# One weight block against a split activation on one Trainium2 core: two matmuls of unequal width, or three of equal width

## The chip, the core and the metric

The kernel runs on one core of a Trainium2 chip. A core has five engines that run their own instruction streams side by side and meet through semaphores: TensorE (PE in the profile; its weight loads have a row of their own, PEld), VectorE (DVE), ScalarE (ACT), GpSimd (POOL) and SyncE (SP, which here issues the transfers from memory). TensorE writes into PSUM, eight banks of 512 float32 columns in each of 128 partitions; everything else lives in SBUF. The metric is the time of one execution on the device, in microseconds (us), and lower is better.

## The reference, cut to what matters

Two decoder layers over 256 tokens with 1024 channels. Each layer is a SwiGLU feed-forward at half weight, a token mixing step, and a second feed-forward, each followed by a layer norm over `alpha * x + sublayer(x)`:

```python
def swiglu(x, w_gate, w_up, w_down):
    return (jax.nn.silu(x @ w_gate) * (x @ w_up)) @ w_down
...
for l in range(DEPTH):
    x = layer_norm(alpha * x + 0.5 * swiglu(x, ffn_w_gate[l, 0], ffn_w_up[l, 0], ffn_w_down[l, 0]), ...)
    u = x @ w_in                                   # conv mixer in layer 0, mLSTM in layer 1
    mix = jnp.concatenate([tok, xa], -1) @ w_out[l]
    x = layer_norm(alpha * x + mix, ...)
    x = layer_norm(alpha * x + 0.5 * swiglu(x, ffn_w_gate[l, 1], ffn_w_up[l, 1], ffn_w_down[l, 1]), ...)
```

The mixer of layer 0 is a gated short convolution, that of layer 1 an mLSTM; in both, a cross-attention into 256 memory tokens runs beside it and the two are concatenated. The feed-forward width is 2816. All of it is float32, and nearly all of the arithmetic is products of a [256, 1024] activation with a weight matrix that is used once.

## The kernel before, in words

To keep float32 accuracy in TensorE's fast float32 format, every operand is split into two exact parts: a rounded high part (ACT copies it, line 99) and the remainder (DVE subtracts, line 100). A product of two split operands is then three products: high by high, high by low and low by high. The weights stream in once from memory, in pieces of [128, 2048] (1 MB), and each piece is split on arrival into `wh` and `wl`; five pieces are held at a time.

There are two ways in which a product is laid out. With the activation stationary (`mm3`, lines 171 to 177), three matmuls of 512 columns each go into the same PSUM columns; the down products (`y`), the output projection (`yo`), the first groups of a feed-forward (`gx`) and the values (`v`) go this way. With the weights stationary (`mmw`, lines 179 to 182), the output comes out transposed, which is what the next product needs; the feed-forward's gate and up products (`gu`), the projections of the mixers (`cg`, `cx`, `cb`, `qkp`), the queries (`xq`) and the memory's keys (`kb`) go this way, a block of 128 by 128 weights at a time.

In `mmw` the activation's two parts lie side by side, 256 tokens each, so one matmul with the high weights covers both parts in 512 columns (line 181): the left half of the PSUM bank gathers high by high, the right half high by low. A second matmul of 256 columns adds the low weights' product to the left half (line 182). After eight such pairs, one for each 128 input channels, the two halves of the bank have to be added: `comb` (lines 184 to 187) lets ACT copy the right half into SBUF, and DVE adds the left half to it. ACT's Silu (line 297), DVE's product of gate and up (line 298) and the split of the result (lines 301 and 302) follow.

A feed-forward has 11 groups of 256 columns. For each of them two pieces hold gate and up, one piece the down weights; `gu_ws` runs four accumulations (`fc` is the half of the group, `m` is gate or up), each into a bank of its own, and the down product of the group before follows. The first group of the first feed-forward is walked chunk by chunk (`outer`), because it starts while its operands are still landing. Each conv, mLSTM or query projection (`proj_ws`) is two accumulations, with `comb` after each. Matmul outputs come from two pools of four PSUM banks, `mbank` and `ybank`; a fifth accumulation waits until the first one's bank has been read. A scheduler decides the order in which each engine's instructions stand, and semaphores are derived from the data; all engines take their instructions in that order.

Of the kernel before, what the change touches and what calls it, by code (L numbers as in the profile page):

```python
# [14 lines left out]
P = 128  # L15
T = 256
# [15 lines left out]
def trunk(ctx: ExitStack, tc: tile.TileContext, d, out):  # L32
# [18 lines left out]
    def mbank(name):  # L51
        return psm.tile([P, 512], F32, tag="mm", name=name)
# [118 lines left out]
    def mm3(o, a, b, start, stop):  # L171
        """o += a^T b with a, b in two exact parts."""
        ah, al = a
        bh, bl = b
        pe.matmul(o, ah, bh, start=start, stop=False)  # L175
        pe.matmul(o, ah, bl, start=False, stop=False)  # L176
        pe.matmul(o, al, bh, start=False, stop=stop)  # L177

    def mmw(bank, w, a, start, stop):
        """bank = [w_h^T a_h + w_l^T a_h | w_h^T a_l], a's parts side by side."""  # L180
        pe.matmul(bank, w[0], a.rearrange("p c t -> p (c t)"), start=start, stop=False)  # L181
        pe.matmul(bank[:, :T], w[1], a[:, 0], start=False, stop=stop)  # L182

    def comb(o, bank):
        """The sum of a bank's two halves."""
        act.activation(o, bank[:, T:], AF.Copy)  # L186
        dve.tensor_add(o, o, bank[:, :T])  # L187
# [76 lines left out]
    def ffn(l, j, xs_groups, i, last=False):  # L264
# [6 lines left out]
        def gu_ws(g, outer=False):  # L271
            w = [get("gu", l, j, g, 0), get("gu", l, j, g, 1)]
            new_h(g)
            banks = {}

            def mm(fc, m, k):
                if k == 0:
                    banks[fc, m] = mbank(f"gu{l}{j}_{g}_{fc}{m}")
                c0 = (k % 4) * 512 + m * 256 + fc * P
                wk = w[k // 4]  # L280
                mmw(banks[fc, m], (wk[0][:, c0:c0 + P], wk[1][:, c0:c0 + P]), cur["x"][:, k],
                    k == 0, k == KC - 1)

            if outer:
                for k in range(KC):
                    for fc in range(2):
                        for m in range(2):
                            mm(fc, m, k)
            for fc in range(2):
                t_ = tmp(f"s{l}{j}_{g}_{fc}")  # L290
# [89 lines left out]
    kvs = {}  # L380

    def mem_kv(mem):
        w = [get("kv", q) for q in range(4)]
        for l in range(2):
            kvs[l] = (consts.tile([P, 2, T], F32, name=f"kT{l}"), consts.tile([P, 2, T], F32, name=f"vm{l}"))
        for c in range(4):
            b = mbank(f"kb{c}")
            for k in range(KC):
                s = slice((k % 2) * D + c * P, (k % 2) * D + (c + 1) * P)
                wk = w[k // 2]  # L390
                mmw(b, (wk[0][:, s], wk[1][:, s]), mem[:, k], k == 0, k == KC - 1)
            comb(kvs[c // 2][0][:, c % 2], b)
# [20 lines left out]
    def proj_to(o, w, name):  # L413
        proj_ws(w, name, lambda c, b: comb(o[:, c * T:(c + 1) * T], b))

    class Xattn:
        def __init__(self, l, w, mix):
            self.l, self.mix = l, mix
            self.kT, self.v = kvs[l]
            self.qT = tmp(f"xqT{l}")  # L420
            self.p = {}

            def use(c, b):
                o = self.qT[:, c * T:(c + 1) * T]
                act.activation(o, b[:, T:], AF.Copy, scale=0.125)
                dve.scalar_tensor_tensor(o, b[:, :T], 0.125, o, op0=ALU.mult, op1=ALU.add)
            proj_ws(w, f"xq{l}", use)
# [84 lines left out]
    def conv_mixer(mix, between):  # L512
        for i in range(3):
            cg = tmp(f"cgs{i}")
            proj_to(cg, get("wc", 1 + 3 * i), f"cg{i}")
            between[i]()
            tt = tmp(f"ct{i}")
            proj_to(tt, get("wc", 2 + 3 * i), f"cx{i}")
            dve.tensor_mul(tt, cg, tt)
# [8 lines left out]
            bt = tmp(f"cb{i}")  # L528
            proj_to(bt, get("wc", 3 + 3 * i), f"cb{i}")
            dve.tensor_mul(r, r, bt)  # L530
# [9 lines left out]
    def mlstm_mixer(mix, i):  # L540
# [3 lines left out]
        # the output gate, natural; the input and forget gates ride along  # L544
# [21 lines left out]
        # gates as rows [head, t]  # L566
# [7 lines left out]
        def gate_rows():  # L574
# [5 lines left out]
            # log_sigmoid(f) = min(f, 0) - log1p(exp(-|f|)); ln(u) is corrected for u's rounding  # L580
# [12 lines left out]
            # running sums and maxima  # L593
# [17 lines left out]
        # decay weights, transposed: E[s, t] = exp(a_s - M_t) for t >= s  # L611
# [12 lines left out]
        # q and k, convolved, silu'd, transposed: [channel, q or k, chunk, t]  # L624
        qk = [hp.tile([P, 2, 2, T], F32, tag="h", name=f"qk{n}") for n in range(3)]

        def qk_piece(n):
# [3 lines left out]
            ut = tmp(f"qu{n}")  # L631

            def use(c, b):
# [8 lines left out]
            proj_ws(get("wm", 1 + n), f"qkp{n}", use)  # L642
# [15 lines left out]
        # h = num / max(|den|, exp(-m)), head norm  # L658
# [32 lines left out]
        # v, natural, with a column of ones after each head  # L691
# [91 lines left out]
def _layouts(i):  # L783
# [5 lines left out]
    def colmajor(w, width):  # L789
        """[1024, n*width] -> [n, 128, 8*width]: piece, k in chunk, chunk x column."""  # L790
# [44 lines left out]
```

## Time and profile before

| what | value |
|---|---|
| median of 3 runs | 1002.04 us (1001.4 to 1003.79) |
| profiled execution, first to last instruction | 1004.1 us, 0.2% above that median |
| busy: PE, PEld, DVE, ACT | 986.8, 834.7, 664.8, 530.1 us |
| PE matmuls | 5116, each with a weight load of its own |
| granted TensorE clock, mean | 0.991 |

The profile has one row for each group of like instructions: the line of the kernel, the engine, the operation, what it writes and reads, how many there are, the busy time, the mean of one and the idle time just before them. The end of a matmul is modelled and matmuls overlap, so the duration of one says little about how fast they follow each other. For that one reads the timeline, which gives the start of each instruction: the distance between two starts is what a matmul costs in a full queue. In the text below this distance is called a slot.

### The profile page before, as it was taken

Reading aid. Unit: us, or ns where it says so; the run is one execution under the profiler, and the core shown is the slowest. Engines: PE = TensorE matmul, PEld = TensorE weight load, DVE = VectorE, ACT = ScalarE, POOL = GpSimd, SP = SyncE. Lnnn points to the kernel's source line nnn. Section 1 sums busy time; section 2 is a strip of 40 time slices with the busy share of each in tenths; the row PEclk is TensorE's granted clock in tenths of the full one; section 3 lists DMA queues with packets and bytes.
Section 4 is the critical chain, followed back from the end, with each engine's and each line's share of the span. In section 5 each row is a group of like instructions: output and inputs, shape, how many; then the busy total and the mean of one; then the engine's idle time right before and its main releaser. Section 6 shows DMA issues by size and latency. Waiting matters only on the chain.

```text
span 1004.1 us, 12980 instructions
## 1 busy us (share of the span) xinstructions
PE 986.8 (98%) x5116; PEld 834.7 (83%) x5116; DVE 664.8 (66%) x1010; ACT 530.1 (53%) x851; POOL 39.4 (4%) x52
## 2 busy tenths in 40 slices
PE   8999999999999999999999999999999999999996
PEld 7888888888888888888788888889788788888885
DVE  6685657868677656565866656576478887556555
ACT  6565555447445545556355555535676346454540
POOL 0000000100000000000100000002300110000001
PEclk9999999999999999999999999999799999999999
DMA  8884546455535654644464646434145466546421
GB/s 277 311 295 166 210 168 212 171 228 205 187 130 187 241 201 159 218 155 180 173 246 168 215 162 213 154 111 154 78 149 205 185 236 230 199 158 216 161 84 43
DMA packets 29293, 186.90 MB, mean 186 GB/s; under 512 B 3632, under 2 KB 4656, under 8 KB 8368
## 3 DMA queue, kind: packets, MB, share of 16 engines
q1 hardware_dynamic: 29232, 186.07, 51.7%
q8 instruction: 40, 0.66, 0.2%
q14 instruction: 21, 0.17, 0.1%
HBM read 185.01 MB, written 1.05 MB: 185 GB/s over the span
## 4 chain that ended last, share of the span: by engine, by line
PE 89%; DVE 4%; POOL 2%; DMA 2%; issue 2%; ACT 0%; SPq 0%; POOLq 0%; DVEq 0%; ACTq 0%
PE gu L181 28%; PE gu L182 14%; PE y L177 8%; PE y L175 8%; PE y L176 8%; PE qkp L181 3%; PE gx L175 2%; PE gx L177 2%; PE gx L176 2%; DVE wl L100 1%; PE qkp L182 1%; PE cx L181 1%; PE cg L181 1%; PE cb L181 1%; PE yo L177 1%
## 5 line engine op out<-in xcount | busy, mean ns | idle before, releaser
L100 DVE TENSOR_TENSOR wl<-raw,wh 128x1024 fp32r<-128x1024 f32 (+1 forms) x342 | 400.6, 1195 | 147.6 <-ACT wh L99 146.8
L181 PE MATMUL gu<-x,wh 128*128 128x512 f32 x1216 | 431.1, 399 | 1.4 <-DVE s L187 1.1
L99 ACT ACTIVATE wh<-raw 128x1024 fp32r<-128x1024 f32 (+1 forms) x342 | 338.3, 1032 | 113.4 <-PE y L177 45.0
L182 PE MATMUL gu<-x,wl 128*128 128x256 f32 x1216 | 340.8, 281 | 0.4 <-DVE wl L100 0.2
L181 PEld LDWEIGHTS gu<-x,wh 128*128 128x128 f32 x1216 | 228.5, 188 | 57.4 <-DVE s L187 1.4
L182 PEld LDWEIGHTS gu<-x,wl 128*128 128x128 f32 x1216 | 230.0, 189 | 2.6 <-DVE wl L100 1.0
L175 PE MATMUL y<-wh,h 128*128 128x512 f32 x352 | 138.1, 392 | 0.0
L177 PE MATMUL y<-wh,h 128*128 128x512 f32 x352 | 137.7, 391 | 0.0
L176 PE MATMUL y<-wl,h 128*128 128x512 f32 x352 | 137.2, 390 | 0.0
L187 DVE TENSOR_TENSOR s<-s,gu 128x256 f32<-128x256 f32 x152 | 63.2, 417 | 107.6 <-ACT s L186 107.6
L186 ACT ACTIVATE s<-gu 128x256 f32<-128x256 f32 x152 | 57.4, 379 | 111.4 <-PE gu L182 110.7
L177 PEld LDWEIGHTS y<-wh,h 128*128 128x128 f32 x352 | 66.1, 188 | 14.5
L175 PEld LDWEIGHTS y<-wh,h 128*128 128x128 f32 x352 | 66.1, 188 | 14.0
L176 PEld LDWEIGHTS y<-wl,h 128*128 128x128 f32 x352 | 66.1, 188 | 13.0
L301 ACT ACTIVATE h<-s 128x256 fp32r<-128x256 f32 x76 | 31.7, 417 | 68.2 <-DVE s L298 68.0
L297 ACT ACTIVATE s<-s 128x256 f32<-128x256 f32 x76 | 31.6, 416 | 37.0 <-DVE s L187 37.0
L302 DVE TENSOR_TENSOR h<-s,h 128x256 fp32r<-128x256 f32 x76 | 32.0, 421 | 17.9 <-ACT h L301 17.9
L181 PE MATMUL qkp<-x,wh 128*128 128x512 f32 x96 | 38.6, 438 | 0.0
L175 PE MATMUL gx<-wh,x 128*128 128x512 f32 x96 | 38.2, 398 | 0.2 <-DVE x L261 0.2
L177 PE MATMUL gx<-wh,x 128*128 128x512 f32 x96 | 37.5, 391 | 0.0
L176 PE MATMUL gx<-wl,x 128*128 128x512 f32 x96 | 37.4, 390 | 0.0
L260 ACT ACTIVATE x<-xt 128x512 fp32r<-128x512 f32 x20 | 11.4, 596 | 44.2 <-PE xt L239 43.8
(191 smaller groups left out, 996.1 us busy)
## 6 DMA issues: line engine op xcount, KB each, us to landing
raw<-in_wgu SPq DMA_DIRECT2D x83, 1024.0 KB, 4.8
raw<-in_wd SPq DMA_DIRECT2D x43, 1024.0 KB, 4.8
raw<-in_wconv SPq DMA_DIRECT2D x10, 1024.0 KB, 4.8
raw<-in_wout SPq DMA_DIRECT2D x8, 1024.0 KB, 4.8
raw<-in_wm SPq DMA_DIRECT2D x7, 1024.0 KB, 4.7
gb<-in_lngb SPq DMA_DIRECT2D x6, 1024.0 KB, 4.9
raw<-in_wkv SPq DMA_DIRECT2D x4, 1024.0 KB, 4.9
raw<-in_wop SPq DMA_DIRECT2D x4, 776.0 KB, 4.2
```

What stands on the lines that cost most here:

```text
L99: act.activation(h, raw, AF.Copy)
L100: dve.tensor_sub(l, raw, h.bitcast(F32))
L175: pe.matmul(o, ah, bh, start=start, stop=False)
L176: pe.matmul(o, ah, bl, start=False, stop=False)
L177: pe.matmul(o, al, bh, start=False, stop=stop)
L181: pe.matmul(bank, w[0], a.rearrange("p c t -> p (c t)"), start=start, stop=False)
L182: pe.matmul(bank[:, :T], w[1], a[:, 0], start=False, stop=stop)
L186: act.activation(o, bank[:, T:], AF.Copy)
L187: dve.tensor_add(o, o, bank[:, :T])
L297: act.activation(t_[:, :256], t_[:, :256], AF.Silu)
L301: act.activation(hh, t_[:, 256:], AF.Copy)
L302: dve.tensor_sub(hT[g][:, 1, fc, :], t_[:, 256:], hh.bitcast(F32))
```

## The change

The weights stay stationary, and the three products of a block become three matmuls of 256 columns into the same 256 columns of PSUM: high weights by high part, high weights by low part, low weights by high part. The sum of all three then stands in PSUM, and `comb` goes away with its ACT copy and its DVE add. Since an accumulation now takes half a bank, gate and up of one half-group share a bank (not in the chunk-by-chunk first group, where four accumulations are open at once and each keeps a bank), and so do the two chunks of each projection. What follows an accumulation reads PSUM itself: Silu, the product of gate and up, the convolutions' multiplications; the copies of two chunks become one of 512 columns. Comments and descriptions are dropped as well.

```diff
-    def mmw(bank, w, a, start, stop):
-        pe.matmul(bank, w[0], a.rearrange("p c t -> p (c t)"), start=start, stop=False)
-        pe.matmul(bank[:, :T], w[1], a[:, 0], start=False, stop=stop)
-
-    def comb(o, bank):
-        act.activation(o, bank[:, T:], AF.Copy)
-        dve.tensor_add(o, o, bank[:, :T])
+    def mmw(o, w, a, start, stop):
+        pe.matmul(o, w[0], a[:, 0], start=start, stop=False)
+        pe.matmul(o, w[0], a[:, 1], start=False, stop=False)
+        pe.matmul(o, w[1], a[:, 0], start=False, stop=stop)
...
             if outer:
+                for fc in range(2):
+                    for m in range(2):
+                        banks[fc, m] = mbank(f"gu{l}{j}_{g}_{fc}{m}")[:, :256]
...
-                for m in range(2):
-                    if not outer:
+                if not outer:
+                    b = mbank(f"gu{l}{j}_{g}_{fc}")
+                    for m in range(2):
+                        banks[fc, m] = b[:, m * 256:(m + 1) * 256]
                         for k in range(KC):
                             mm(fc, m, k)
-                    comb(t_[:, m * 256:(m + 1) * 256], banks[fc, m])
-                    if m == 0:
-                        act.activation(t_[:, :256], t_[:, :256], AF.Silu)
-                dve.scalar_tensor_tensor(t_[:, 256:], t_[:, :256], 0.5, t_[:, 256:],
+                act.activation(t_[:, :256], banks[fc, 0], AF.Silu)
+                dve.scalar_tensor_tensor(t_[:, 256:], t_[:, :256], 0.5, banks[fc, 1],
                                          op0=ALU.mult, op1=ALU.mult)
...
-    def proj_ws(w, name, use):
+    def proj_ws(w, name):
+        b = mbank(name)
         for c in range(2):
-            b = mbank(f"{name}_{c}")
             for k in range(KC):
                 s = slice(k * 256 + c * P, k * 256 + (c + 1) * P)
-                mmw(b, (w[0][:, s], w[1][:, s]), cur["x"][:, k], k == 0, k == KC - 1)
-            use(c, b)
+                mmw(b[:, c * T:(c + 1) * T], (w[0][:, s], w[1][:, s]), cur["x"][:, k],
+                    k == 0, k == KC - 1)
+        return b
...
-            proj_to(cg, get("wc", 1 + 3 * i), f"cg{i}")
+            act.activation(cg, proj_ws(get("wc", 1 + 3 * i), f"cg{i}"), AF.Copy)
...
-                comb(ut[:, o:o + 256], b)
-                act.activation(r[:, o:o + 256], ut[:, o:o + 256], AF.Copy, scale=w[3])
+                act.activation(r[:, o:o + 256], b[:, o:o + 256], AF.Copy, scale=w[3])
                 for q, sh in ((0, 3), (1, 2), (2, 1)):
-                    dve.scalar_tensor_tensor(r[:, o + sh:o + 256], ut[:, o:o + 256 - sh], w[q],
+                    dve.scalar_tensor_tensor(r[:, o + sh:o + 256], b[:, o:o + 256 - sh], w[q],
                                              r[:, o + sh:o + 256], op0=ALU.mult, op1=ALU.add)
```

The first place is on PE, in group 9 of a feed-forward in the middle of the program, where the accumulation of gate in the second half-group ends and that of up begins. A row gives the line, the operation, what it writes and reads, and the width. `gu_9_10` is group 9, second half-group, gate; `gu_9_11` is up; `wh` and `wl` are a weight piece's two parts, `x` the activation. Before:

```order
L181 MATMUL gu_9_10_3905<-x_2562,wh_3813 128x512
L182 MATMUL gu_9_10_3905<-x_2562,wl_3814 128x256
L181 MATMUL gu_9_10_3905<-x_2562,wh_3845 128x512
L182 MATMUL gu_9_10_3905<-x_2562,wl_3846 128x256
...
L181 MATMUL gu_9_11_3925<-x_2562,wh_3813 128x512
L182 MATMUL gu_9_11_3925<-x_2562,wl_3814 128x256
```

And of the changed kernel at the same place, where `gu_9_1` is the one bank of the second half-group:

```order
L181 MATMUL gu_9_1_4449<-x_2941,wh_4346 128x256
L182 MATMUL gu_9_1_4449<-x_2941,wh_4346 128x256
L183 MATMUL gu_9_1_4449<-x_2941,wl_4347 128x256
L181 MATMUL gu_9_1_4449<-x_2941,wh_4378 128x256
L182 MATMUL gu_9_1_4449<-x_2941,wh_4378 128x256
L183 MATMUL gu_9_1_4449<-x_2941,wl_4379 128x256
```

Each pair has become three rows of 256 columns, the first two of them with the same stationary block, and gate and up write one bank; over the whole program that is 1520 pairs, 1520 more matmuls and the same number of columns.

The second place is on DVE, between the first and the second group of the very first feed-forward. `wl` rows are splits of arriving weights, `s` is the half-group's SBUF tile, `h` its split result. Before:

```order
L100 TENSOR_TENSOR wl_183<-raw_181,wh_182 128x1024
L187 TENSOR_TENSOR s_0_0_259<-s_0_0_259,gu_0_00_191 128x256
L187 TENSOR_TENSOR s_0_0_259<-s_0_0_259,gu_0_01_194 128x256
L100 TENSOR_TENSOR wl_183<-raw_181,wh_182 128x1024
L298 SCALAR_TENSOR_TENSOR s_0_0_259<-s_0_0_259 128x256
L187 TENSOR_TENSOR s_0_1_268<-s_0_1_268,gu_0_10_197 128x256
L187 TENSOR_TENSOR s_0_1_268<-s_0_1_268,gu_0_11_200 128x256
L302 TENSOR_TENSOR h_0_190<-s_0_0_259,h_0_190 128x256
```

And of the changed kernel:

```order
L100 TENSOR_TENSOR wl_183<-raw_181,wh_182 128x1024
L295 SCALAR_TENSOR_TENSOR s_0_0_291<-s_0_0_291,gu_0_01_192 128x256
L100 TENSOR_TENSOR wl_183<-raw_181,wh_182 128x1024
L299 TENSOR_TENSOR h_0_190<-s_0_0_291,h_0_190 128x256
L295 SCALAR_TENSOR_TENSOR s_0_1_296<-s_0_1_296,gu_0_11_194 128x256
```

The four adds of `comb` (line 187) are gone, the product of gate and up now reads the bank itself, and the first group's banks are released by Silu on ACT (gate) and by this product on DVE (up).

More of the change, by code (lines that the diff above doesn't have):

```diff
@@ L276, in mm @@
             def mm(fc, m, k):
-                if k == 0:
-                    banks[fc, m] = mbank(f"gu{l}{j}_{g}_{fc}{m}")
                 c0 = (k % 4) * 512 + m * 256 + fc * P
@@ L385, in mem_kv @@
             kvs[l] = (consts.tile([P, 2, T], F32, name=f"kT{l}"), consts.tile([P, 2, T], F32, name=f"vm{l}"))
[L386 to L392, printed above, removed]
+        for l in range(2):
+            b = mbank(f"kb{l}")
+            for c in range(2):
+                for k in range(KC):
+                    c0 = (k % 2) * D + (2 * l + c) * P
+                    wk = w[k // 2]
+                    mmw(b[:, c * T:(c + 1) * T], (wk[0][:, c0:c0 + P], wk[1][:, c0:c0 + P]),
+                        mem[:, k], k == 0, k == KC - 1)
+            act.activation(kvs[l][0].rearrange("p c t -> p (c t)"), b, AF.Copy)
         pending()
@@ L402, in mem_kv @@
                 act.activation(kvs[l][1][:, c], b[:, l * 256:(l + 1) * 256], AF.Copy)
-    def proj_ws(w, name, use):
+    def proj_ws(w, name):
+        b = mbank(name)
         for c in range(2):
-            b = mbank(f"{name}_{c}")
             for k in range(KC):
                 s = slice(k * 256 + c * P, k * 256 + (c + 1) * P)
-                mmw(b, (w[0][:, s], w[1][:, s]), cur["x"][:, k], k == 0, k == KC - 1)
-            use(c, b)
-    def proj_to(o, w, name):
-        proj_ws(w, name, lambda c, b: comb(o[:, c * T:(c + 1) * T], b))
+                mmw(b[:, c * T:(c + 1) * T], (w[0][:, s], w[1][:, s]), cur["x"][:, k],
+                    k == 0, k == KC - 1)
+        return b
     class Xattn:
@@ L421, in __init__ @@
             self.p = {}
[L423 to L427, printed above, removed]
+            act.activation(self.qT, proj_ws(w, f"xq{l}"), AF.Copy, scale=0.125)
         def scores(self, c):
@@ L514, in conv_mixer @@
             cg = tmp(f"cgs{i}")
-            proj_to(cg, get("wc", 1 + 3 * i), f"cg{i}")
+            act.activation(cg, proj_ws(get("wc", 1 + 3 * i), f"cg{i}"), AF.Copy)
             between[i]()
             tt = tmp(f"ct{i}")
-            proj_to(tt, get("wc", 2 + 3 * i), f"cx{i}")
-            dve.tensor_mul(tt, cg, tt)
+            dve.tensor_mul(tt, cg, proj_ws(get("wc", 2 + 3 * i), f"cx{i}"))
             r = tmp(f"cr{i}")
@@ L527, in conv_mixer @@
                                              r[:, o + sh:o + 256], op0=ALU.mult, op1=ALU.add)
-            bt = tmp(f"cb{i}")
-            proj_to(bt, get("wc", 3 + 3 * i), f"cb{i}")
-            dve.tensor_mul(r, r, bt)
+            dve.tensor_mul(r, r, proj_ws(get("wc", 3 + 3 * i), f"cb{i}"))
             rv = r.rearrange("p (c t) -> p c t", c=2)
@@ L630, in qk_piece @@
             r = tmp(f"qr{n}")
-            ut = tmp(f"qu{n}")
-            def use(c, b):
+            b = proj_ws(get("wm", 1 + n), f"qkp{n}")
+            for c in range(2):
                 o = c * 256
-                comb(ut[:, o:o + 256], b)
                 w = [qcw[:, 6 * which + 2 * i + c, q:q + 1] for q in range(4)]
-                act.activation(r[:, o:o + 256], ut[:, o:o + 256], AF.Copy, scale=w[3])
+                act.activation(r[:, o:o + 256], b[:, o:o + 256], AF.Copy, scale=w[3])
                 for q, sh in ((0, 3), (1, 2), (2, 1)):
-                    dve.scalar_tensor_tensor(r[:, o + sh:o + 256], ut[:, o:o + 256 - sh], w[q],
+                    dve.scalar_tensor_tensor(r[:, o + sh:o + 256], b[:, o:o + 256 - sh], w[q],
                                              r[:, o + sh:o + 256], op0=ALU.mult, op1=ALU.add)
-            proj_ws(get("wm", 1 + n), f"qkp{n}", use)
             act.activation(qk[i][:, which].rearrange("p c t -> p (c t)"), r, AF.Silu)
```

## The prediction

> **What bounds the kernel now.** I read the page first, for the engine that is never idle.
>
> ```profile
> span 1004.1 us, 12980 instructions
> PE 986.8 (98%) x5116; PEld 834.7 (83%) x5116; DVE 664.8 (66%) x1010; ACT 530.1 (53%) x851; POOL 39.4 (4%) x52
> PEclk9999999999999999999999999999799999999999
> PE 89%; DVE 4%; POOL 2%; DMA 2%; issue 2%; ACT 0%; SPq 0%; POOLq 0%; DVEq 0%; ACTq 0%
> ```
>
> PE is busy for 98% of the span and makes up 89% of the chain that ended last; DVE and ACT have a third and a half of the span to spare. The clock is granted in full except in one of the 40 slices. Next, the waits, to see whether PE ever waits for what the change removes:
>
> ```profile
> PE warm L148 <- ACT warm L145: 2.3, 1, 2.3
> PE tk L715 <- DVE og L712: 1.6, 2, 0.9
> PE xt L239 <- DVE xnat L229: 1.5, 3, 0.7
> PE gu L181 <- DVE s L187: 1.1, 1, 1.1
> ```
>
> These are PE's four longest waits, and only the last names `comb` (L187): a single wait of 1.1 us, at the start of the second weight group. So `comb` is off the path, and the time is the sum of PE's slots. A busy figure doesn't give a slot, since its ends are modelled. I therefore took slots from PE's timeline, over long stretches without a wait. A whole feed-forward group from its second pair to its last, 30 pairs apart:
>
> ```profile
> 328.96 0.40 PE L181 MATMUL gu<-x,wh 128*128 128x512 f32 x1
> 329.19 0.28 PE L182 MATMUL gu<-x,wl 128*128 128x256 f32 x1
> 329.31 0.40 PE L181 MATMUL gu<-x,wh 128*128 128x512 f32 x1
> ...
> 339.56 0.40 PE L181 MATMUL gu<-x,wh 128*128 128x512 f32 x1
> ```
>
> 10.60 us / 30 = 353.3 ns for a pair. In the convolution's projections, 19 pairs apart:
>
> ```profile
> 236.28 0.39 PE L181 MATMUL cx<-x,wh 128*128 128x512 f32 x1
> ...
> 242.87 0.39 PE L181 MATMUL cg<-x,wh 128*128 128x512 f32 x1
> ```
>
> 6.59 us / 19 = 346.8 ns: the same pair, with nothing in its way. To learn what a matmul of 256 columns costs I need the part of a slot that doesn't depend on the width. Two chains of one width give it, one of 512 columns with 20 slots and one of 384 with 19:
>
> ```profile
> 323.62 0.39 PE L175 MATMUL gx<-wh,x 128*128 128x512 f32 x1
> 323.84 0.40 PE L176 MATMUL gx<-wl,x 128*128 128x512 f32 x1
> 324.08 0.39 PE L177 MATMUL gx<-wh,x 128*128 128x512 f32 x1
> ...
> 328.16 0.39 PE L177 MATMUL gx<-wh,x 128*128 128x512 f32 x1
> ```
>
> ```profile
> 704.64 0.34 PE L175 MATMUL v<-wh,x 128*128 128x384 f32 x1
> ...
> 707.94 0.33 PE L176 MATMUL v<-wl,x 128*128 128x384 f32 x1
> ```
>
> 4.54 us / 20 = 227.0 ns and 3.30 us / 19 = 173.7 ns. The 128 columns between them cost 53.3 ns, or 0.4165 ns a column; 512 columns are 213.2 ns, and 13.8 ns of the slot are left over, whatever the width. The undisturbed pair says the same: 768 columns are 319.9 ns, and 346.8 - 319.9 = 26.9 ns are two fixed parts of 13.5.
>
> **The change part by part.** *The matmuls.* The columns stay, 768 a block. What is added is one fixed part: 319.9 + 3 x 13.5 = 360.3 ns, or 120 ns for each 256 columns. The counts:
>
> ```profile
> L181 PE MATMUL gu<-x,wh 128*128 128x512 f32 x1216 | 431.1, 399 | 1.4 <-DVE s L187 1.1 <-ACT wh L99 0.3
> L181 PE MATMUL qkp<-x,wh 128*128 128x512 f32 x96 | 38.6, 438 | 0.0
> L181 PE MATMUL cx<-x,wh 128*128 128x512 f32 x48 | 17.3, 399 | 0.0
> L181 PE MATMUL xq<-x,wh 128*128 128x512 f32 x32 | 11.4, 398 | 0.0
> L181 PE MATMUL kb<-memT,wh 128*128 128x512 f32 x32 | 11.0, 393 | 0.0
> ```
>
> With `cg` and `cb` (48 each, as many as `cx`) that is 1216 + 304 = 1520 pairs. Some are run while the clock is at a half. The first row is the table of stretches (after the stretch PE's busy time, then PEld, DVE, ACT and POOL, and the granted clock, 0.50), the other two are PE's timeline in it:
>
> ```profile
> 717.30:731.00 13.70, 13.70 (x38) 9.61 (x37) 8.74 (x24) 8.04 (x25) 0.00 (x0) 0.50 0.00 0
> ```
>
> ```profile
> 719.05 0.63 PE L181 MATMUL qkp<-x,wh 128*128 128x512 f32 x1
> 719.69 0.63 PE L181 MATMUL qkp<-x,wh 128*128 128x512 f32 x1
> ```
>
> There a pair takes 640 ns, which is 768 columns at half the rate and no fixed part at all; three matmuls take the same 640. The stretch holds 38 matmuls, of which some 28 are 14 pairs, so 14 of the 304 add nothing. Of the 1216 I leave out 16 of the first group, which wait for their operands to land. That gives 1200 x (360.3 - 353.3) = 8.4 us and 290 x (360.3 - 346.8) = 3.9 us, together **+12.3 us** on the path, since nothing else bounds these stretches.
>
> *The weight loads.* Each matmul has a load of its own, also where the block is the one already loaded. Of three `mm3` matmuls the first two share their stationary block, yet each has a load, and the second's slot above (323.84 to 324.08) is as long as the first's:
>
> ```profile
> L176 PEld LDWEIGHTS y<-wl,h 128*128 128x128 f32 x352 | 66.1, 188 | 13.0
> ```
>
> The loads' own rows of the timeline, near the start:
>
> ```profile
> 18.04 0.19 PEld L182 LDWEIGHTS gu<-x,wl 128*128 128x128 f32 x1
> 18.27 0.19 PEld L181 LDWEIGHTS gu<-x,wh 128*128 128x128 f32 x1
> 18.39 0.19 PEld L182 LDWEIGHTS gu<-x,wl 128*128 128x128 f32 x1
> ```
>
> So 1520 loads are added. A load's row says 0.19 us, but the next one follows 0.12 us later where a 256-column matmul runs (18.27 to 18.39), so loads of 0.12 us apart are possible, and that is just the new slot. Whether they hold that pace three in a row and for whole groups no row shows; the nearest is two in a row:
>
> ```profile
> 44.00 0.40 PE L182 MATMUL gu<-x,wl 128*128 128x256 f32 x2
> 44.24 0.40 PE L181 MATMUL gu<-x,wh 128*128 128x512 f32 x1
> ...
> 243.10 0.28 PE L182 MATMUL cg<-x,wl 128*128 128x256 f32 x1
> 243.21 0.39 PE L181 MATMUL cg<-x,wh 128*128 128x512 f32 x1
> ```
>
> Two 256-column matmuls with a load each take 0.24 us, 0.12 apiece. From below the bound is the shortest 256-column slot among these rows, 0.11 us (243.10 to 243.21); from above it is the disturbed pair of the feed-forward, whose matmuls cost (353.3 - 346.8) / 2 = 3.3 ns more than the fixed part, so 123.4 ns. I take 120: it is what chains of one width give, and the new stream has one width.
>
> The Trainium skill ("TensorE: Matmul & The Clock Gate", section "Back-to-back issue gap") gives a warm gap of the columns over 2.4 GHz plus 2.5 ns; by it a pair is 325.0 ns, three matmuls are 327.5, and the matmuls' term would be an estimated +3.7 us. The trace agrees with its rate per column and not with its constant: 13.5 ns stand in the rows, and I go by them.
>
> *`comb`.* In the feed-forwards alone 152 of ACT's copies and 152 of DVE's adds go:
>
> ```profile
> L187 DVE TENSOR_TENSOR s<-s,gu 128x256 f32<-128x256 f32 x152 | 63.2, 417 | 107.6 <-ACT s L186 107.6
> L186 ACT ACTIVATE s<-gu 128x256 f32<-128x256 f32 x152 | 57.4, 379 | 111.4 <-PE gu L182 110.7
> ```
>
> That is 63.2 us of DVE and 57.4 us of ACT, hidden behind PE except for the one wait of 1.1 us. There PE wants the first bank back, and DVE is behind a weight split. In the changed order Silu on ACT frees that bank without DVE, but the second block's low weights still come from the same split, and the bank of `up` is freed by DVE behind it. I take two thirds of the wait, **-0.7 us** (bounds 0 and -1.1). Nothing is queued behind the longer accumulations that PE would wait for: a group's `h` is needed one group later. Should that cover go, the delay of one DVE product, 0.417 us, in each of 152 / 4 = 38 groups would be the price, 16 us; the 34% of the span that DVE is idle speak against it.
>
> *Sum:* +12.3 - 0.7 = +11.6 us, or 1004.1 to 1015.7 for the profiled execution. That execution lies 2.1 us above the median of the runs (1002.0), so the median goes to **1013.6 us**.
>
> **The rivals.** *The uneven stream (slower by more).* The load comes so close to the slot that the delay which the feed-forward's pairs show today falls on each of the three matmuls. Then a block costs 370.2 ns, and 1200 x 16.9 + 290 x 23.4 = 27.1 us; less 0.7, the median is 1028. For it: the disturbed pairs are most of the kernel. Against: both chains of one width run clean, and the disturbance stands only where the width alternates.
>
> *The short slot (faster).* A 256-column matmul may cost less than a third of a pair once no wide one stands beside it. The point from which this decides is 353.3 / 3 = 117.8 ns. At the 0.11 us of the shortest row a block costs 330 ns, which gives 1200 x -23.3 + 290 x -16.8 = -32.8 us and, with the start, 968.5 us; at 115 ns it is 345, -10.5 us and 991. For it: such slots occur. Against: the wide slot beside a short one is longer, so that no pair of a long stretch falls below two fixed parts.
>
> *The cheap third matmul (no change).* The second matmul meets its own block in the array already, and the half-clock stretch shows that the fixed part can be hidden altogether. If the third matmul adds only half of it, a block costs 353.5 ns: 1200 x 0.2 + 290 x 6.7 - 0.7 = +1.5 us, 1003.5. If it adds nothing, it is 346.8, -7.8 - 0.7 us, and 993.5. The slots of `mm3` with their repeated block speak against both. The skill's small constant belongs here, at an estimated 1005.
>
> *The slow stretch.* The half clock from 717 to 731 us costs 6.8 us against the full one. If the new stream shifts PE's activity enough for it to be granted in full, the time is 1006.8; if it comes back one more time, 1020. What stands ahead of that stretch, the mLSTM's gates with their small products, isn't touched by the change, so I expect it to stay.
>
> **How the numbers follow.** Chances: the forecast 0.64, the uneven stream wholly or in part 0.16, the slow stretch otherwise 0.05, the third matmul at half its price or the like 0.09, the short slot or a third matmul for nothing 0.06. The range reaches from 1006 (the slow stretch gone) to 1029 (the uneven stream), and leaves out the two last cases. A change of 0.3%, 3 us, is about what a measurement of this kernel can tell. Faster 0.06, the same 0.09, slower 0.85.
>
> **What would show it.** In the changed profile the start of the first `gu` matmul to that of the last in a group, over the blocks between, should give 360 ns, and a 256-column slot 0.12 us; at 0.115 the short slot is right, at 0.123 the uneven stream. A second slot (L182) shorter than the first would show the free repeat. PEld should count 6636, DVE's busy time fall by 63 us or more, and the wait of `gu` L181 shrink while the other waits of PE stay. If the span grows by less than 8 us with slots of 120 ns, PE has lost a stall that I didn't see; if PE waits for ACT or DVE in the groups, `comb` had a use.

## The result, and the profile after

| what | before | after |
|---|---|---|
| median, lowest and highest (4 runs each, in turn on one chip) | 1001.72 us (1000.32 to 1003.79) | 1011.77 us (1010.53 to 1013.38) |
| ratio, with its 95% interval | | 1.0103 (1.0084 to 1.0122) |
| span of the profiled execution | 1004.1 us | 1011.6 us |
| granted clock of the profiled execution, mean | 0.991 | 0.996 |

The change makes the kernel slower by 10.05 us, with an interval of 8.4 to 12.2 us; +11.6 had been forecast. The page of the changed kernel shows what became of each engine:

```profile
span 1011.6 us, 15642 instructions
PE 994.2 (98%) x6636; PEld 914.0 (90%) x6636; DVE 596.1 (59%) x820; ACT 459.1 (45%) x668; POOL 38.2 (4%) x52
PEclk9999999999999999999999999999999999999999
```

The matmuls are the 5116 of before plus the 1520 that were counted. DVE has lost 68.7 us of work and ACT 71.0, and the kernel is slower all the same: PE is still busy for 98% of the span, as it was before, so this share tells nothing of the loss. A loss on an engine that is always busy has to be read from the distance between starts. PE's timeline in the same feed-forward group as before, from the second block to the last:

```profile
334.74 0.28 PE L181 MATMUL gu<-x,wh 128*128 128x256 f32 x1
334.86 0.28 PE L182 MATMUL gu<-x,wh 128*128 128x256 f32 x1
334.98 0.28 PE L183 MATMUL gu<-x,wl 128*128 128x256 f32 x1
...
345.54 0.28 PE L181 MATMUL gu<-x,wh 128*128 128x256 f32 x1
...
345.90 0.38 PE L327 MATMUL hx<-ident,sx 128*128 128x128 f32 x2
346.04 0.48 PE L175 MATMUL y<-wh,h 128*128 128x512 f32 x1
346.36 0.40 PE L176 MATMUL y<-wl,h 128*128 128x512 f32 x1
...
347.95 0.39 PE L177 MATMUL y<-wh,h 128*128 128x512 f32 x1
```

10.80 us / 30 = 360.0 ns a block, in three even slots of 120; before, the pair took 353.3. The matmul on L182 meets the block that L181 has just used and is no cheaper. The last rows show something that I had not looked for. The seven down matmuls from 346.36 to 347.95 take 227.1 ns each. At the same place the kernel before still runs uneven, after its last pair:

```profile
340.36 0.39 PE L176 MATMUL y<-wl,h 128*128 128x512 f32 x1
340.59 0.40 PE L177 MATMUL y<-wh,h 128*128 128x512 f32 x1
340.83 0.39 PE L175 MATMUL y<-wh,h 128*128 128x512 f32 x1
341.06 0.40 PE L176 MATMUL y<-wl,h 128*128 128x512 f32 x1
341.29 0.39 PE L177 MATMUL y<-wh,h 128*128 128x512 f32 x1
```

0.93 us / 4 = 232.5 ns. So the pairs cost something behind them as well. In this group two transposes (`hx`) stand between `gu` and `y`. In the 26 groups in which 24 `y` follow `gu` directly, both kernels begin `y` with long slots: some ten before, mostly 63 ns together above the 227, and five after, 28 ns together. Next, what PE waits for, longest first (total, times, longest):

```profile
PE warm L148 <- ACT warm L145: 2.3, 1, 2.3
PE tk L701 <- DVE og L698: 1.6, 2, 0.9
PE xt L235 <- DVE xnat L225: 1.6, 4, 0.6
PE gu L183 <- DVE wl L100: 1.4, 4, 0.5
PE gu L181 <- ACT wh L99: 0.8, 1, 0.8
```

The wait for `comb` is gone, and waits for the splits of arriving weights, 2.2 us together where they were 0.5, stand in its place. Last, the half clock, in the table of stretches:

```profile
726.80:730.20 3.40, 3.40 (x16) 3.23 (x16) 3.14 (x13) 3.06 (x14) 0.00 (x0) 0.50 0.00 0
```

It lasts 3.4 us here where it lasted 13.7 in the profile of before. Adding up PE's distances from start to start over the whole of both profiled executions gives the difference of the spans (us):

| part | before | after | difference |
|---|---|---|---|
| weight-stationary matmuls behind the first `y`, without the stage of the mLSTM's gates | 507.9 | 520.4 | +12.5 |
| `mm3` matmuls (`y`, `yo`, `gx`, `v`, `vb`, `op`) outside that stage | 394.5 | 393.2 | -1.3 |
| mLSTM's gates: first `grows` to the first `xo` behind it | 29.3 | 24.5 | -4.8 |
| first matmul to the first `y` | 29.3 | 30.3 | +1.0 |

Together +7.4, of a difference of 7.5.

### The profile page after: what moved, and what is told of

Same layout as the page of the kernel before. It is cut to its first block, busy times and chain, and to the rows that moved or that the text cites. A ratio compares the mean times of both kernels' runs of the same rounds, so it can differ in the third digit from the quotient of the medians.

```text
span 1011.6 us, 15642 instructions
## 1 busy us (share of the span) xinstructions
PE 994.2 (98%) x6636; PEld 914.0 (90%) x6636; DVE 596.1 (59%) x820; ACT 459.1 (45%) x668; POOL 38.2 (4%) x52
## 4 chain that ended last, share of the span: by engine, by line
PE 88%; DVE 3%; DMA 3%; POOL 2%; issue 2%; ACT 1%; POOLq 0%; DVEq 0%; SPq 0%; ACTq 0%
PE gu L183 14%; PE gu L182 14%; PE gu L181 14%; PE y L177 7%; PE y L175 7%; PE y L176 7%; DMA raw<-in_wgu 3%; PE gx L177 2%; PE gx L176 2%; PE gx L175 2%; PE qkp L183 1%; PE qkp L181 1%; PE qkp L182 1%; PE xt L235 1%; PE yo L177 1%
## 5 line engine op out<-in xcount | busy, mean ns | idle before, releaser
L183 PE MATMUL gu<-x,wl 128*128 128x256 f32 x1216 | 344.5, 284 | 1.5 <-DVE wl L100 1.4
L181 PE MATMUL gu<-x,wh 128*128 128x256 f32 x1216 | 344.5, 283 | 0.9 <-ACT wh L99 0.8
L182 PE MATMUL gu<-x,wh 128*128 128x256 f32 x1216 | 343.9, 283 | 0.0
L181 PEld LDWEIGHTS gu<-x,wh 128*128 128x128 f32 x1216 | 233.3, 192 | 2.6 <-ACT wh L99 1.4
L183 PEld LDWEIGHTS gu<-x,wl 128*128 128x128 f32 x1216 | 233.1, 192 | 2.6 <-DVE wl L100 2.5
L182 PEld LDWEIGHTS gu<-x,wh 128*128 128x128 f32 x1216 | 233.3, 192 | 1.1
L294 ACT ACTIVATE s<-gu 128x256 f32<-128x256 f32 x76 | 28.4, 374 | 128.4 <-PE gu L183 128.4
L295 DVE SCALAR_TENSOR_TENSOR s<-s,gu 128x256 f32<-128x256 f32 x76 | 31.8, 418 | 89.1 <-ACT s L294 89.1
L176 PEld LDWEIGHTS y<-wl,h 128*128 128x128 f32 x352 | 66.2, 188 | 12.5
L299 DVE TENSOR_TENSOR h<-s,h 128x256 fp32r<-128x256 f32 x76 | 32.1, 422 | 17.9 <-ACT h L298 17.9
```

Of the source, the lines that this page charges most:

```text
L181: pe.matmul(o, w[0], a[:, 0], start=start, stop=False)
L182: pe.matmul(o, w[0], a[:, 1], start=False, stop=False)
L183: pe.matmul(o, w[1], a[:, 0], start=False, stop=stop)
L294: act.activation(t_[:, :256], banks[fc, 0], AF.Silu)
L295: dve.scalar_tensor_tensor(t_[:, 256:], t_[:, :256], 0.5, banks[fc, 1], op0=ALU.mult, op1=ALU.mult)
```

## The experiments

Three questions were open: whether the matmuls make the whole loss or `comb` has a share in it; what sets the 120 ns; and what the unevenness of the pairs is, since a kernel without it would beat both. The theory is a fixed part of 13.5 ns for each matmul, with `comb` hidden. Its rivals are a cost that comes from the reading of PSUM or the sharing of banks, a limit of the weight loads at 120 ns, and a loss in the half-clock stretch.

**The wide matmul cut, all else as before.** `comb` and the two halves stay.

```diff
-        pe.matmul(bank, w[0], a.rearrange("p c t -> p (c t)"), start=start, stop=False)
+        pe.matmul(bank[:, T:], w[0], a[:, 1], start=start, stop=False)
+        pe.matmul(bank[:, :T], w[0], a[:, 0], start=False, stop=False)
         pe.matmul(bank[:, :T], w[1], a[:, 0], start=False, stop=stop)
```

> The kernel before with one half of the change: the 512-column matmul is cut into two of 256, each into its own half of the bank, and comb stays as it is. If each matmul carries a fixed part of 13.5 ns and comb is hidden behind TensorE, this one costs as much as the whole change: 1010 to 1014 us, with 360 ns for a block of three. If taking comb away had given time back, it lies above 1015. If the whole change is slow for another reason, such as gate and up sharing a bank, it lies near the kernel before, 1001 to 1004.

1013.91 us (1012.39 to 1016.64), ratio 1.0134 (1.0117 to 1.0150). PE's timeline in the same group, second block to last:

```profile
333.70 0.28 PE L181 MATMUL gu<-x,wh 128*128 128x256 f32 x1
...
344.49 0.28 PE L181 MATMUL gu<-x,wh 128*128 128x256 f32 x1
```

10.79 us / 30 = 359.7 ns. The cut alone makes the whole loss, and what the change does to PSUM and to the readers isn't needed for it. Its ratio lies 0.0031 above that of the changed kernel, or 3 us, so both ran again, in one set of rounds:

> The run with three matmuls and comb kept, once more, beside the changed kernel in the same rounds, since their ratios to the kernel before, 1.0134 and 1.0102, were taken on different occasions. If comb's removal is worth 2 to 3 us beside the longer stream, this one again lies 2 to 3 us above the changed kernel: 1013 to 1015 against 1010.5 to 1012. If the difference was only the draw of the half-clock stretch, the two lie within 1 us.

> The changed kernel in the same rounds: 1010.5 to 1012 either way; what counts is its distance to the run with comb kept, 2 to 3 us or under 1.

The cut alone gave 1013.10 us (ratio 1.0130, 1.0109 to 1.0151), the changed kernel 1012.99 (ratio 1.0117, 1.0102 to 1.0132). An earlier repeat of the changed kernel:

> The changed kernel, unchanged, beside the other three on one chip, to weigh it against the run that split the matmuls and kept comb (ratio 1.0134 to the kernel before). If comb is worth nothing beside the longer stream, this ratio is 1.013 as well; if its removal gives back 1 to 3 us, as the first measurement of this kernel (1.0103) suggests, it is 1.010 to 1.012.

1011.38 us, ratio 1.0102 (1.0087 to 1.0116). The medians of the two kernels are 0.1 us apart in the shared rounds, and their intervals overlap. What `comb` is worth beside the longer stream lies between nothing and some 3 us, and these times don't fix it further. The profiles show one place: at the start of the second group PE waits 1.4 and 1.3 us for `comb` in the two profiles of the cut alone, and 0.5, 0.5 and 0 us for weight splits in the three of the changed kernel. That is about 1 us.

**`comb` alone taken away.** The pairs stay; Silu and the product read the left half of each bank; in the projections the add goes, and a copy of the left half stays. This leaves out the product of the high weights with the activation's low part, which is still computed but not added.

```diff
     def comb(o, bank):
-        act.activation(o, bank[:, T:], AF.Copy)
-        dve.tensor_add(o, o, bank[:, :T])
+        act.activation(o, bank[:, :T], AF.Copy)
...
-                    comb(t_[:, m * 256:(m + 1) * 256], banks[fc, m])
                     if m == 0:
-                        act.activation(t_[:, :256], t_[:, :256], AF.Silu)
+                        act.activation(t_[:, :256], banks[fc, 0][:, :T], AF.Silu)
-                dve.scalar_tensor_tensor(t_[:, 256:], t_[:, :256], 0.5, t_[:, 256:],
+                dve.scalar_tensor_tensor(t_[:, 256:], t_[:, :256], 0.5, banks[fc, 1][:, :T],
...
```

> The kernel before with the other half alone: the pairs of 512 and 256 columns stay, and what follows reads the left half of the bank, so the product of high weights and low activation is left out of the sum and comb's ACT copies and DVE adds are gone. If comb is hidden, the time is that of the kernel before less at most 1 us: 1000 to 1003. If comb holds TensorE up somewhere that the waits do not show, it is 998 or less.

999.65 us (12 runs), ratio 0.9991 (0.9982 to 1.0000): between 0 and 1.8 us. From its page and its timeline:

```profile
PE 980.9 (98%) x5116; PEld 831.8 (83%) x5116; DVE 595.0 (60%) x820; ACT 472.0 (47%) x699; POOL 37.2 (4%) x52
```

```profile
326.74 0.40 PE L181 MATMUL gu<-x,wh 128*128 128x512 f32 x1
...
337.34 0.40 PE L181 MATMUL gu<-x,wh 128*128 128x512 f32 x1
```

DVE is rid of 69.8 us and ACT of 58.1, and the pair still takes 10.60 us / 30 = 353.3 ns. `comb` was hidden but for what these 0 to 1.8 us hold, and it isn't what makes the pairs uneven.

**Two matmuls of 128 columns for the third.** Were there only a fixed part, a block would grow by one more of them, to 374 ns; a limit of the loads would show in the short slots.

```diff
-        pe.matmul(o, w[1], a[:, 0], start=False, stop=stop)
+        pe.matmul(o[:, :P], w[1], a[:, 0, :P], start=False, stop=False)
+        pe.matmul(o[:, P:], w[1], a[:, 0, P:], start=False, stop=stop)
```

> The changed kernel with the third matmul of each block cut into two of 128 columns, to see how near a slot of 120 ns is to the pace of the weight loads. If only the fixed part counts, a slot of 128 columns is 53.3 + 13.5 = 67 ns, a block 374 ns, and the time 1011 + 1490 x 13.6 ns = some 1031 us. If a load needs about 109 ns, the pace of the 128-column transposes, a block is 458 ns and the time some 1158 us. If a load needs the full 120 ns, so that the changed stream runs at the loads' limit, a block is 480 ns and the time some 1190 us.

One run: 1182.17 us. PE's timeline over four blocks:

```profile
400.12 0.33 PE L181 MATMUL gu<-x,wh 128*128 128x256 f32 x1
400.29 0.28 PE L182 MATMUL gu<-x,wh 128*128 128x256 f32 x1
400.41 0.22 PE L183 MATMUL gu<-x,wl 128*128 128x128 f32 x1
400.47 0.28 PE L184 MATMUL gu<-x,wl 128*128 128x128 f32 x1
400.58 0.33 PE L181 MATMUL gu<-x,wh 128*128 128x256 f32 x1
...
401.97 0.33 PE L181 MATMUL gu<-x,wh 128*128 128x256 f32 x1
```

1.85 us / 4 = 462.5 ns a block, where the same columns and four fixed parts would be 374. One slot of 128 columns takes 0.06 us, and the next two, 0.11 and 0.17, pay it back. The loads' own rows show where the block loses its time:

```profile
400.17 0.19 PEld L182 LDWEIGHTS gu<-x,wh 128*128 128x128 f32 x1
400.29 0.19 PEld L183 LDWEIGHTS gu<-x,wl 128*128 128x128 f32 x1
400.41 0.19 PEld L184 LDWEIGHTS gu<-x,wl 128*128 128x128 f32 x1
400.52 0.19 PEld L181 LDWEIGHTS gu<-x,wh 128*128 128x128 f32 x1
400.63 0.19 PEld L182 LDWEIGHTS gu<-x,wh 128*128 128x128 f32 x1
```

Two loads in each block are followed by the next after 0.12 us, the slot of a 256-column matmul, and two after 0.11 (111 to 113 ns unrounded). The shorter distance is the pace of the loads when the matmuls are short: 2 x 120 + 2 x 111.5 = 463. So beneath some 112 ns a matmul no longer hides its load. The 120 ns of the changed kernel are set by the fixed part, with 8 ns to spare. The block agrees with the expectation for loads of about 109 ns (458); the whole time lies nearer to the 1190 us of 120 ns, but this execution also holds half-clock stretches of 6.8, 10.2 and 3.4 us.

**Fewer changes of width.** In the kernel before, each pair changes the width twice. This kernel runs the eight wide matmuls of an accumulation first, and then the eight narrow ones; the same matmuls, in another order (the walk by chunks at the start is left as it was).

```diff
+    def mmws(bank, wx):
+        for k0 in range(0, KC, 8):
+            for k in range(k0, k0 + 8):
+                w, a = wx(k)
+                pe.matmul(bank, w[0], a.rearrange("p c t -> p (c t)"), start=k == 0, stop=False)
+            for k in range(k0, k0 + 8):
+                w, a = wx(k)
+                pe.matmul(bank[:, :T], w[1], a[:, 0], start=False, stop=k == KC - 1)
```

> The kernel before with the same matmuls in another order: in each accumulation the eight matmuls of 512 columns first, then the eight of 256. If the 6.5 ns by which a feed-forward pair exceeds two fixed parts come from widths that alternate, a group of eight costs 8 x (227 + 120) = 2776 ns in place of 2826, which is 150 x 50 ns = 7.5 us: 992 to 996. If they come from how dense the loads are or from the other engines' traffic, the time stays at 1000 to 1003. If each change of width restarts the same unrest as the first y matmuls after a group show, some 50 ns for eight, the gain is eaten up: 1000 to 1003 as well, but with uneven slots in the wide chains.

994.96 us (6 runs), ratio 0.9948 (0.9934 to 0.9963). Its timeline, in which the trace joins matmuls that overlap (the count stands last in a row):

```profile
400.73 2.00 PE L188 MATMUL gu<-x,wh 128*128 128x512 f32 x8
402.57 1.11 PE L191 MATMUL gu<-x,wl 128*128 128x256 f32 x8
403.53 2.00 PE L188 MATMUL gu<-x,wh 128*128 128x512 f32 x8
```

2.80 us / 8 = 350 ns a block instead of 353.3, with 1.84 / 8 = 230 ns for the wide slot and 0.96 / 8 = 120 for the narrow one. (The rows are rounded to 10 ns. Over whole groups, from the first of 32 blocks to what follows the last, the median of 28 groups is 348.3 ns a block here and 352.8 before.) The wide slots one by one, behind the step from narrow to wide, are 233, 236, 228, 233, 231, 226, 227 and 227 ns: the first five are disturbed. The narrow ones behind the other step are 113, 119 and then 120. If only such steps cost, one per group should be better still. So the next kernel runs all 32 wide matmuls of a group's four accumulations and then the 32 narrow ones (and both chunks of a projection likewise):

```diff
+    def mmws(jobs):
+        for bank, wx in jobs:
+            for k in range(KC):
+                w, a = wx(k)
+                pe.matmul(bank, w[0], a.rearrange("p c t -> p (c t)"), start=k == 0, stop=False)
+        for bank, wx in jobs:
+            for k in range(KC):
+                w, a = wx(k)
+                pe.matmul(bank[:, :T], w[1], a[:, 0], start=False, stop=k == KC - 1)
```

> The kernel before with the wide matmuls of all four accumulations of a feed-forward group first (32 in a row), then all 32 narrow ones, and in the projections those of both chunks. If a step from narrow to wide costs some 21 ns net wherever it stands, and only there, three of the four steps in a group go: 37 groups x 64 ns and 19 projections x 21 ns, together 2.8 us below the order by single accumulations (994.96), so 991 to 993.5. If the unrest comes from the number of narrow matmuls in a row, it stays at 994 to 996. If the four banks, held until the group's end, make TensorE wait, it is above 996 with waits for ACT or DVE in the groups.

```profile
396.90 7.42 PE L188 MATMUL gu<-x,wh 128*128 128x512 f32 x32
404.15 4.00 PE L192 MATMUL gu<-x,wl 128*128 128x256 f32 x32
407.99 0.40 PE L175 MATMUL y<-wh,h 128*128 128x512 f32 x1
...
408.92 0.39 PE L176 MATMUL y<-wl,h 128*128 128x512 f32 x1
```

In the group it does what was expected: 7.25 us / 32 = 226.6 ns and 3.84 / 32 = 120.0, so 346.6 a block, and the one step left disturbs the `y` behind it (0.93 us / 4 = 232.5). The time missed its expectation: 994.61 us, ratio 0.9941 (0.9929 to 0.9953). The span shows where: from the mLSTM's first `xo` to its first `num` it takes 48.2 us where before took 45.9, and from there to the last feed-forward 32.1 where before took 30.8. Its waits name only a small part of that, one of 0.6 us of `xo` for ACT that the kernel before doesn't have. That a projection hands its results on late when its two chunks end together is likely, and not shown.

The other direction, two wide and two narrow in turn (`range(0, KC, 2)`, and runs of 2), keeps a step in every second block:

> The kernel before with two wide matmuls, then two narrow ones, in turn. If every step from a narrow to a wide matmul upsets the slots that follow it, as the order by accumulations showed (233, 236, 228, 233, 231 after eight narrow ones), two blocks cost 2 x 347 + 7 + 10 - 7 = some 704 ns or 352 each, hardly below the 353 of single pairs: 999 to 1001 us. If it is the share of matmuls with a step that counts in proportion, half the excess goes: 350 ns and some 996 us.

```profile
399.52 0.63 PE L188 MATMUL gu<-x,wh 128*128 128x512 f32 x2
399.99 0.39 PE L191 MATMUL gu<-x,wl 128*128 128x256 f32 x2
...
402.31 0.40 PE L188 MATMUL gu<-x,wh 128*128 128x512 f32 x1
```

2.79 us / 8 = 349 ns a block, below both values expected (348.0 over whole groups): four steps in eight blocks cost no more than one. A price per step, the idea behind this kernel, is refuted. The slots one by one show how: the wide ones are all long (233, 236, 232, 231), but each train ends after two of them, and the narrow ones behind are short (115, 113, 114, 119). Its one run took 990.09 us; six more gave:

> The order by twos once more, now timed: its one look gave 990.09 us in an execution without a half-clock stretch, with 348 ns a block where 352 were expected. If the slots are what counts, 1200 blocks at 5 ns less and 290 at 347 to 349 give 6 us against the kernel before, and the median lies at 993 to 996 beside 1000 to 1001, level with the order by whole accumulations. If the order by twos saves elsewhere too, in the mLSTM, where the wider groupings hold their banks longer, it lies at 990.5 to 993. If the one look was luck with the stretch alone, 996 or more.

992.09 us (990.18 to 992.79, 6 runs) against 1001.06 us, ratio 0.9910 (0.9893 to 0.9926). It beats both kernels, with the matmuls of the kernel before in another order. Against the profile of before, the weight-stationary matmuls take 5.9 us less, the `mm3` matmuls 1.9, the stretch ahead of the first `y` 2.2, and the gates' stage, with 3.4 us of half clock for 13.7, 4.3. In its profile the mLSTM stage takes 45.9 us and the one behind it 30.6, as before: the chunks still end one after the other.

**The half-clock stretch.** Since the gates' stage gave back 4.8 us in the profile after, I tried to cover it: a block of query and key projections ahead of the gates' columns, and one decay later.

```diff
+        qk_piece(0)
         columns()
         decay(0)
-        decay(2)
-        qk_piece(0)
         xa.values(0)
         qk_piece(1)
+        decay(2)
```

> The kernel before with the first q and k projection of the mLSTM put ahead of the gates' columns and decay products, and the second decay product later, so that dense matmuls stand where TensorE ran small ones and waited. If the half-clock stretch follows from that sparse place, it is gone from the profile and the time is 2 to 5 us lower, 995.5 to 998.5, and spreads less. If the stretch has another cause, the time stays at 999.5 to 1002 and a stretch of half clock stands somewhere in the mLSTM.

1005.15 us (6 runs), ratio 1.0043 (1.0030 to 1.0056): slower, and above both ranges expected. Its profile has no stretch in this place (clock 0.998), but among PE's waits it has new ones:

```profile
PE pT L463 <- DVE cols L608: 1.5, 1, 1.5
...
PE tk L715 <- DVE dn L676: 0.9, 1, 0.9
PE xo L468 <- ACT p L465: 0.7, 1, 0.7
```

The stage behind the gates took 49.9 us instead of 45.9. Those 4.0 us are more than half clock for 3.4 us costs (1.7), and less than it cost in the profile of before (13.7 / 2 = 6.9). Together with the 32 wide matmuls in a row it was no better:

> Both reorderings together, on the pairs of the kernel before. If they are independent, their gains add: some 8 us for the widths and 2 to 5 for the gates, 987 to 991. If the gates' place costs the same whatever the order, 991 to 993.

997.32 us, ratio 0.9965 (0.9953 to 0.9977); that stage took 54.1 us, and a stretch of 3.4 us stands in it. Nor can the missing stretch be put down to the edit. With the gates' stage in its old order, the profiles show 13.7 us (before), 10.2 (the third matmul cut in two), 6.8 and two times 3.4 (three profiles of the changed kernel), 3.4 (five others), and none (the 32 in a row, and the first run of two and two). The changed kernel's three and the two of the same order by twos show that the length differs between executions of one program.

## Why the prediction was right, point by point

**PE bounds it, and `comb` is off the path: right.** Taking `comb` alone away is worth 0.9 us, with an interval of 0 to 1.8, near the 0.7 that I took for its wait.

**The block at 360.3 ns: right.** Measured were 360.0 in the changed kernel and 359.7 in the cut alone. The term was forecast at +12.3 us; the 48 blocks of it that lie ahead of the first `y` (64 there, 16 left out) are 0.3 of that, so 12.0 stand against the +12.5 measured for the rest. The rivals by which a block costs less or more fall with the same slots: 120, 120 and 120 ns. The third matmul isn't cheap, a short slot of 0.11 us is only what a neighbour lends, and the disturbance of the pairs doesn't go over to a stream of one width. The Trainium skill ("TensorE: Matmul & The Clock Gate", section "Back-to-back issue gap") has 2.5 ns, for an isolated matmul, as the part that doesn't depend on the width; the trace differs, with 120 - 106.6 = 13.4 ns (256 columns at 0.4165 ns), and by that page the term would have been the estimated +3.7 us of the prediction.

**Loads 0.12 us apart for whole groups: right, with little to spare.** With a fourth load in each block the loads became the bound for its short matmuls, at some 112 ns.

**The start at -0.7 us: right for the wait, and not seen in the sum.** Where PE waited 1.1 us for `comb`, at the first matmul of the second group, it now waits two matmuls further on for the low weights:

```profile
19.58 0.28 PE L182 MATMUL gu<-x,wh 128*128 128x256 f32 x1
20.35 0.38 PE L183 MATMUL gu<-x,wl 128*128 128x256 f32 x1 [0.49 <-DVE wl L100]
```

So this wait is 0.6 us shorter. The prediction had named that split as what is late next and counted a third of the wait for it; it is 0.49 us of 1.12. All the same the stretch ahead of the first `y` grew by 1.0 us in this profile, and 0.95 of it is there from the first matmul on:

```profile
6.80 0.39 PE L181 MATMUL gu<-x,wh 128*128 128x256 f32 x1 [0.75 <-ACT wh L99]
```

Before, the first `gu` started at 5.85 us: the first weight piece came later, which the sum didn't have. From the first `gu` to the first `y` both kernels take 25.8 us. In the two other profiles of the changed kernel the stretch ahead of the first `y` takes 29.4 and 29.8 us, against 29.3 before, so the size of this row changes from one execution to the next.

**The stretch of half clock "expected to stay": it stayed in place and not in length.** 3.4 us in place of 13.7 accounts for the -4.8 us of that stage, since a microsecond at half clock costs about half of one (a pair takes 640 ns in it and some 347 outside): 10.3 / 2 = 5.2. Of the four rivals this is the one that came true in part, in this profile. It wasn't the new stream's doing, as the same length stands in profiles with the pairs. It also explains most of why the profiles differ by 7.5 us and the medians by 10.05: the profiled execution of before was one with a long stretch (its clock 0.991, that of the 11 later runs beside the first repeat 0.994 to 0.997) and lay some 3.9 us above its median, the one after 1.6 us. The prediction had a sign for this case, a span that grows by less than 8 us with slots of 120 ns, and read it as a stall that PE has lost. It came true, and what PE had lost was half clock.

**Not foreseen:** the `mm3` matmuls gained 1.3 us. Of this `y` has 1.1, and 0.9 of that stands in the 26 groups where `y` follows `gu` directly: its long slots are fewer, five for ten, and not gone.

**A slip that cost nothing:** I held the span of before, 1004.1 us, against the median of the times. A run of the changed kernel took 1013.38 us for a span of 1011.6, so 1.8 us lie around the span, and the profiled execution of before lay some 3.9 us above its median and not 2.1. The sum was a difference and doesn't hang on it. Nor does it hang on the count in the half-clock stretch: it holds 16 wide and 15 narrow matmuls of `qkp`, so 15 pairs or a little more, where I took 14; each moves the sum by 0.013 us.

What stays open: why a step from narrow to wide disturbs the slots behind it, and why fewer of them when fewer narrow ones stand ahead of it. And the share of `comb` beside the longer stream: 0 to 3 us by the times, of which the waits show about 1.

## What to carry to other kernels

Where PE is busy from end to end and a change leaves the columns as they are, count the matmuls: here each cost 13.4 ns beside its columns, and taking 69 us off DVE and 71 off ACT paid for little or nothing of the 1520 that were added. Take that price from distances between starts in long stretches of one width, and the disturbance of mixed widths from the mixed stretch itself; the order alone (two wide, two narrow) was worth 9 us here, nearly as much as the change lost. Before a stall is counted as a gain, look at which operand arrives next behind it.

## What the runs showed of the hardware that was not expected

- A step from 256 to 512 columns disturbs the slots behind it, whether they belong to `gu` or to `y`: five behind eight narrow matmuls or more (233, 236, 228, 233 and 231 ns instead of 227), two behind two (233 and 231), some ten in `y` behind a group of pairs. A step from 512 to 256 shows no long slots but short ones (113 and 119 instead of 120). Over whole groups a block costs 352.8 ns in pairs, 348.3 by eights, 348.0 by twos and 346.4 by 32.
- A matmul of 128 columns can follow after 0.06 us, but its neighbours then take 0.11 and 0.17: its load follows the one before no faster than in some 112 ns. A load of the block that is already there is not spared (slots of 120, 120 and 120 ns).
- The half-clock stretches in the gates' stage lasted nothing, 3.4, 6.8, 10.2 or 13.7 us with the code of that stage in one order, and differed between executions of one program (3.4 and 6.8 in the changed kernel, none and 3.4 by twos). The Trainium skill ("TensorE: Matmul & The Clock Gate", section "What's actually happening") has a free-running window of 3.4 us behind the clock; the trace agrees, with lengths of 0, 1, 2, 3 and 4 such windows. Each window more makes a profile some 1.7 us longer; whether a kernel's code has a part in how many there are, these runs don't show.
- The first weight piece reached ACT at 5.14 to 6.12 us in the five profiles of the two kernels with 6636 matmuls, and at 4.34 to 4.79 us in the nine others, the one with the most matmuls among them. Its loads are the same; what delays it wasn't found.
